# Last projection of a two-layer recurrent trunk: token parts of 384 and 128, and another way to 1/rms

## The chip, the cores and the metric

The kernel runs on one core of a Trainium2 chip. The metric is the time of one execution on the device in microseconds (us). A core has a matrix engine (TensorE, PE in the profile; its weight loads are PEld), a vector engine (VectorE, DVE), a scalar engine (ScalarE, ACT), a general one (GpSimd, POOL), and SyncE (SP), which here issues the transfers between the chip's memory and the core's SBUF. Matmuls write into PSUM, in banks of 512 fp32 columns.

## What is computed

A trunk of two layers over 512 tokens of width 2048, with residual adds and a final RMSNorm. The change lies at the very end, in layer 1's output projection, its residual add and the final norm:

```python
x = x + ssd_layer(rmsnorm(x, o_norm[j]), ...)   # ends in: return y @ w_out, y: 512 x 4096, w_out: 4096 x 2048
return rmsnorm(x, final_norm)

def rmsnorm(x, w):
    y = xf * lax.rsqrt(jnp.mean(xf * xf, axis=-1, keepdims=True) + EPS)
    return y * w
```

The mean is over the 2048 features of one token, and the whole product must be known for a token before any of its features can be scaled.

## The kernel before

Everything is held transposed: features on the 128 partitions, tokens along the free axis. The residual `x` is `acc_t`, 16 column tiles (`acc[0]` to `acc[15]`) of 128 features by 512 tokens. A weight matrix comes from memory in fp32, and ScalarE and VectorE split it into a rounded part and the rest (`split`, L167 to L169), both in the type fp32r; the moving operand is split likewise. `mm3` (L146 to L150) then multiplies with three matmuls: high by high, high by low, low by high. Each of the three loads its 128 x 128 weights first. Matmuls on plain fp32 tiles stand in the trace as two instructions each.

Layer 1 works through eight groups of features. The output projection of a group, 512 of the 4096 inputs, is added into `acc` while the next group is computed (`outproj`). For the last group nothing follows that could hide it, and so it is written apart, from L890 to the end of `trunk`:

- The 16 weight tiles `wl` are loaded and split ahead of time.
- `out_tile(j, lo, hi)` makes 12 matmuls (four input tiles times three) for column tile `j` and tokens `lo` to `hi` into a PSUM bank `po`, adds them to `acc[j]` (`evac`, VectorE, L217), squares the result (ScalarE, L910), adds the squares into `ssq2` (L912), and multiplies `acc[j]` by its norm weight (ScalarE, L915).
- Column tiles 0 to 7 (`FULL`) go over all 512 tokens, and GpSimd adds their squares. Tiles 8 to 15 then go over tokens 0 to 255, and after that over 256 to 511; VectorE adds those squares.
- After each half a matmul with a matrix of ones sums `ssq2` over the partitions and puts the sum on all of them (`rs`, L925 and L926). ScalarE takes the root (`std`, L928), VectorE the reciprocal of 128 x 256 values in two pieces (L180), and then VectorE scales the 16 tiles in five products (L933), each followed by a transfer of 256 or 512 KB to `out`.

The first half's scaling and output run while TensorE does the second half. Each engine runs its instructions in one order, fixed when the program is built; a tile framework adds the waits. `evac` is placed with high priority, so on VectorE the adds of the second half stand between the products of the first. All transfers of the end go through SyncE's one queue, in program order: a transfer whose data are not ready holds up those behind it.

Of the kernel before, what the change touches and what calls it, by code (L numbers as in the profile page):

```python
# [9 lines left out]
F32 = mybir.dt.float32  # L10
F32R = mybir.dt.float32r
AF = mybir.ActivationFunctionType
# [4 lines left out]
P = 128  # L17
S = 512
D = 2048
KD = D // P  # L20
# [23 lines left out]

VB = (2, 2)

FULL = 8

WARM = 7
QS = [(6, 10)] * (NG - 1) + [(4, 6)]  # L50
# [3 lines left out]
def trunk(ctx, tc, x_t, par, w_in0, w_qkvo, w_lru, w_if, w_out0, w_in1, w_out1, out):  # L54
    nc = tc.nc
    v, sc, gp, pe = nc.vector, nc.scalar, nc.gpsimd, nc.tensor
    MUL, ADD, SUB, MAX, MIN = ALU.mult, ALU.add, ALU.subtract, ALU.max, ALU.min
# [7 lines left out]
    def dma(o, i):  # L65
        return nc.sync.dma_start(o, i)
# [3 lines left out]
    def pc(name, j=0, n=1):  # L70
        o = OFF[name][0] + j
        return prm[:, o:o + n]

    ident = pc("ident", 0, 128)
    mask = pc("mask", 0, 128)
    eps = cst.tile([P, 1], F32, name="eps")
# [4 lines left out]
    aiT = cst.tile([P, 16], F32, name="aiT")  # L81
# [3 lines left out]
    r_bc = cst3.tile([P, S], F32, name="r_bc")  # L85
    acc_t = cst3.tile([P, KD, S], F32, name="acc")
    acc = [acc_t[:, k] for k in range(KD)]
# [5 lines left out]
    ones = ones_r.bitcast(F32)  # L93
# [5 lines left out]
    def next_raw():  # L99
        raw_i[0] += 1  # L100
        return raws[raw_i[0] % len(raws)]
# [44 lines left out]
    def mm3(ps, w, mov, first, last):  # L146
        (wh, wl), (mh, ml) = w, mov
        pe.matmul(ps, wh, mh, start=first, stop=False)  # L148
        pe.matmul(ps, wh, ml, start=False, stop=False)  # L149
        pe.matmul(ps, wl, mh, start=False, stop=last)  # L150
# [20 lines left out]
    def mmt(name="mm"):  # L171
        return pmm.tile([P, S], F32, tag="mm", name=name)

    def axt(name="ax"):
        return pax.tile([P, S], F32, tag="ax", name=name)


    def recip(dst, src, w=S):
        for o in range(0, w, P):
            v.reciprocal(dst[:, o:o + P], src[:, o:o + P])  # L180
# [34 lines left out]
    def evac(o, a, b, op):  # L215
        with tc.high_priority(offset=1000):
            v.tensor_tensor(o, a, b, op=op)  # L217
# [41 lines left out]
    def st(name="s", dt=F32):  # L259
        return sp[0].tile([P, S], dt, tag="s", name=name, bufs=sp[1])  # L260
# [30 lines left out]
    for k in range(KD):  # L291
# [10 lines left out]
        hi = wp.tile([P, 512], F32R, tag="whi", name="whi", bufs=4)  # L302
        lo = wp.tile([P, 512], F32R, tag="wlo", name="wlo", bufs=4)
        o = 512 * (k % 2)
# [17 lines left out]
        for w, m in ((hi, xh), (hi, xl), (lo, xh)):  # L322
            for t in range(4):
                pe.matmul(ps01[t], w[:, t * P:(t + 1) * P], m[k], start=(k == 0 and w is hi and m is xh),
                          stop=(k == KD - 1 and w is lo))
# [10 lines left out]
    def xslot(name):  # L336
        return (PA.tile([P, S], F32R, tag="yh", name=name + "h", bufs=8),
                PA.tile([P, S], F32R, tag="yl", name=name + "l", bufs=8))
# [17 lines left out]
    for h in range(NH):  # L356
        xm, xc = [], []
        for t in range(4):
            j = 4 * h + t
            if h:  # L360
                ps = mmt("xm")
                proj(ps, w_in0[16 + j], xpairs)
            else:
                ps = ps01[j]
# [288 lines left out]
    ps = mmt("dt")  # L653
    wdt = []
    for c in range(2):
        with tc.high_priority(offset=3000):
            w = next_raw()[:, 3:]
# [4 lines left out]
    hs = [(slice(64 * e, 64 * e + 64), slice(256 * e, 256 * e + 256)) for e in range(2)]  # L662
# [12 lines left out]
    def lt(tag, bufs=1, shape=(P, S), dt=F32):  # L675
        return L1.tile(list(shape), dt, tag=tag, name=tag, bufs=bufs)
# [211 lines left out]
    wl = []  # L888
# [1 line left out]
        wl += load_w(w_out1[j // 2, NG - 1], (xpairs[j], xpairs[j + 1]) if j < KD - 2 else (None, None))  # L890


    H = S // 2
    ssq2 = st("ssq2")
    sqs = {}

    def out_tile(j, lo, hi):
        n = hi - lo
        pst = mmt("po")
        for kk in range(4):  # L900
            ks = slice(kk * P, (kk + 1) * P)
            y = prev["out"][kk]
            mm3(pst[:, :n], (wl[j][0][:, ks], wl[j][1][:, ks]), (y[0][:, lo:hi], y[1][:, lo:hi]), kk == 0, kk == 3)
        a = acc[j][:, lo:hi]
        evac(a, a, pst[:, :n], ADD)
        if j == 0:
            sc.activation(ssq2, a, AF.Square)
        else:
            sq = st("sq")[:, :n]
            sc.activation(sq, a, AF.Square)  # L910
            if j < KD - 1:
                (gp if n == S else v).tensor_tensor(ssq2[:, lo:hi], ssq2[:, lo:hi], sq, op=ADD)  # L912
            else:
                sqs[lo] = sq
        sc.mul(a, a, pc("f_norm", j))  # L915

    for j in range(FULL):
        out_tile(j, 0, S)
    for hf in range(2):
        hs = slice(hf * H, (hf + 1) * H)  # L920
        for j in range(FULL, KD):
            out_tile(j, hf * H, (hf + 1) * H)
        r = r_bc[:, hs]
        ps = axt("rs")
        pe.matmul(ps[:, :H], ones, ssq2[:, hs], start=True, stop=False)  # L925
        pe.matmul(ps[:, :H], ones, sqs[hf * H], start=False, stop=True)  # L926
        std = st("std")[:, :H]
        sc.activation(std, ps[:, :H], AF.Sqrt, bias=eps, scale=1.0 / D)  # L928
        recip(r, std, H)
        done = 0  # L930
        for n in (4, 4, 4, 2, 2):
            a = acc_t[:, done:done + n, hs]
            v.tensor_tensor(a, a, r.unsqueeze(1).to_broadcast([P, n, H]), op=MUL)  # L933
            dma(out[hf, :, done:done + n], a)
            done += n


def _cm(vec):
# [93 lines left out]
```

## Time and profile before

| | |
|---|---|
| median of 3 runs | 2637.56 us (2636.6 to 2639.3) |
| the profiled execution | 2636.36 us |
| its span, first to last instruction | 2634.5 us |
| mean granted TensorE clock | 0.998 |
| column tile 4 of the last projection begins | 2584.38 us |
| tile 8, tokens 0 to 255, begins | 2595.26 us |
| last matmul of the projection starts | 2619.32 us |
| first scaled product of the second half starts | 2625.34 us |

Times inside the execution are counted from the start of its span. In the groups of instructions the figures behind the bar are the total busy time in us, the mean of one in ns, and the idle time just before them with what ended it. "x6" counts instructions. Matmuls are pipelined: their records overlap, so the distance from one start to the next, not the record's length, is what one costs.

### The profile page before, as it was taken

How to read it: one execution, taken by the hardware profiler on the slowest of the kernel's cores; microseconds unless marked ns; L12 is line 12 of the kernel's file. 1: busy time of each engine (PE TensorE's matmuls, PEld its weight loads, DVE VectorE, ACT ScalarE, POOL GpSimd, SP SyncE). 2: the span in 40 equal slices, each digit the busy share in tenths (PEclk: the TensorE clock that was granted, in tenths of full speed). 3: DMA queues.
4: the chain of work that ended last, by engine and by line, in shares of the span. 5: the costliest groups of instructions: out<-in, count | busy, mean ns of one | idle time of the engine just before them, and what ended most of it. 6: DMA issues, size and time to landing. Idle time of an engine off the chain costs nothing.

```text
span 2634.5 us, 32622 instructions
## 1 busy us (share of the span) xinstructions
PE 2619.1 (99%) x12246; PEld 2147.1 (81%) x12246; DVE 1642.9 (62%) x2708; ACT 1190.4 (45%) x1846; POOL 97.8 (4%) x86
## 2 busy tenths in 40 slices
PE   9999999999999999999999999999999999999997
PEld 8887878788888888888888888888888888888887
DVE  8452534487757757665767666666666666666676
ACT  6443443477436446453554334343343333343435
POOL 1000000000000000000200000000000000000001
PEclk9999999999999999999999999999999999999999
DMA  5424242533333323332253332323333333233332
GB/s 184 137 96 144 96 136 96 161 102 129 113 106 112 115 102 108 102 108 96 85 132 113 104 120 96 120 101 108 112 101 115 105 104 120 90 123 101 107 104 105
DMA packets 114910, 297.18 MB, mean 113 GB/s; under 512 B 11960, under 2 KB 35256, under 8 KB 114752
## 3 DMA queue, kind: packets, MB, share of 16 engines
q1 hardware_dynamic: 114608, 294.83, 34.0%
q8 instruction: 97, 1.59, 0.2%
q14 instruction: 61, 0.50, 0.1%
q10 hardware_dynamic: 144, 0.26, 0.0%
HBM read 277.99 MB, written 17.06 MB: 112 GB/s over the span
## 4 chain that ended last, share of the span: by engine, by line
PE 99%; DMA 0%; DVE 0%; ACT 0%; SPq 0%; issue 0%; DVEq 0%
PE po L148 9%; PE po L149 9%; PE po L150 9%; PE xbc L148 7%; PE xbc L150 7%; PE xbc L149 7%; PE z L148 4%; PE z L150 4%; PE z L149 4%; PE xl L148 2%; PE xl L149 2%; PE zm L148 2%; PE zm L149 2%; PE xl L150 2%; PE zm L150 2%; PE zl L150 2%
## 5 line engine op out<-in xcount | busy, mean ns | idle before, releaser
L168 ACT CAST whi<-wraw 128x512 fp32r<-128x512 f32 (+1 forms) x881 | 541.3, 615 | 1073.8 <-PE po L149 285.1
L169 DVE TENSOR_TENSOR wlo<-wraw,whi 128x512 fp32r<-128x512 f32 (+1 forms) x881 | 622.5, 707 | 520.2 <-ACT whi L168 490.3
L148 PE MATMUL xbc<-xh,whi 128*128 128x512 f32 x768 | 300.9, 392 | 0.0
L150 PE MATMUL xbc<-xh,wlo 128*128 128x512 f32 x768 | 299.0, 389 | 0.0
L149 PE MATMUL xbc<-xl,whi 128*128 128x512 f32 x768 | 298.9, 389 | 0.0
L217 DVE TENSOR_TENSOR acc<-acc,po 128x512 f32<-128x512 f32 (+1 forms) x264 | 175.8, 666 | 187.7 <-PE po L150 186.9
L148 PE MATMUL z<-xh,whi 128*128 128x512 f32 x512 | 206.9, 404 | 0.0
L150 PE MATMUL z<-xh,wlo 128*128 128x512 f32 x512 | 199.8, 390 | 0.0
L149 PE MATMUL z<-xl,whi 128*128 128x512 f32 x512 | 199.3, 389 | 0.0
L148 PE MATMUL po<-yh,whi 128*128 128x512 f32 (+1 forms) x456 | 179.4, 393 | 0.0
L150 PE MATMUL po<-yh,wlo 128*128 128x512 f32 (+1 forms) x456 | 176.9, 388 | 0.0
L149 PE MATMUL po<-yl,whi 128*128 128x512 f32 (+1 forms) x456 | 176.7, 388 | 0.0
L148 PEld LDWEIGHTS xbc<-xh,whi 128*128 128x128 f32 x768 | 144.2, 188 | 30.6 <-issue 1.2
L150 PEld LDWEIGHTS xbc<-xh,wlo 128*128 128x128 f32 x768 | 144.2, 188 | 30.1
L149 PEld LDWEIGHTS xbc<-xl,whi 128*128 128x128 f32 x768 | 144.2, 188 | 29.5
L235 POOL TENSOR_TENSOR ssq<-ssq,sq 128x512 f32<-128x512 f32 x51 | 65.9, 1292 | 1598.1 <-ACT sq L234 1598.1
L150 PEld LDWEIGHTS z<-xh,wlo 128*128 128x128 f32 x512 | 96.1, 188 | 20.9
L149 PEld LDWEIGHTS z<-xl,whi 128*128 128x128 f32 x512 | 96.3, 188 | 20.5 <-issue 1.9
L148 PEld LDWEIGHTS z<-xh,whi 128*128 128x128 f32 x512 | 96.3, 188 | 20.4 <-issue 2.1
L148 PE MATMUL zl<-xh,whi 128*128 128x512 f32 x256 | 101.5, 396 | 0.0
L148 PE MATMUL po<-ylh,whi 128*128 128x512 f32 x256 | 100.9, 394 | 0.0
L150 PEld LDWEIGHTS po<-yh,wlo 128*128 128x128 f32 x456 | 85.6, 188 | 18.0
(342 smaller groups left out, 5216.6 us busy)
## 6 DMA issues: line engine op xcount, KB each, us to landing
wraw<-in_w_in_dram SPq DMA_DIRECT2D x287, 512.0 KB, 3.2
wraw<-in_w_out_dram SPq DMA_DIRECT2D x128, 512.0 KB, 3.2
dab<-dad SPq DMA_DIRECT2D x64, 256.0 KB, 3.2
wraw<-in_w_qkvo_dram SPq DMA_DIRECT2D x24, 512.0 KB, 3.2
E<-ed SPq DMA_DIRECT2D x64, 128.0 KB, 2.9
vd<-vn SPq DMA_DIRECT2D x16, 256.0 KB, 3.7
od<-zm SPq DMA_DIRECT2D x16, 256.0 KB, 3.8
V<-vd SPq DMA_DIRECT2D x16, 256.0 KB, 3.9
```

The source lines that it names most:

```text
L148: pe.matmul(ps, wh, mh, start=first, stop=False)
L149: pe.matmul(ps, wh, ml, start=False, stop=False)
L150: pe.matmul(ps, wl, mh, start=False, stop=last)
L168: last_hi[:] = [sc.copy(hi, src)]
L169: return v.tensor_tensor(lo, src, hi.bitcast(F32), op=SUB)
L217: v.tensor_tensor(o, a, b, op=op)
L235: eng.tensor_tensor(ssq, ssq, sq, op=ADD)
```

## The change

Up to column tile 3 of the last projection every engine's order is as before. From there:

- `FULL` is 4 and a new constant `TA` is 384. Column tiles 0 to 3 go over 512 tokens, tiles 4 to 15 over tokens 0 to 383, all in one loop; GpSimd adds the squares of both.
- Tokens 384 to 511 of tiles 4 to 15 come last, in three groups of four column tiles. A group shares one PSUM bank, 128 columns for each tile, and has one add, one square (`ssqB`, `sqB`) over 512 columns and four products with the norm weight.
- The sum of squares is taken with the squares as weights and one column of ones as the moving operand (`r_sum`): the sums stand with tokens on partitions, one column for every 128 tokens. The squares of the last tiles go into it directly. Root and reciprocal work on 3 columns (first part) or 1 (second).
- `r_rows` brings 1/rms back to rows: ScalarE scales the identity by it (`dg`), and a matmul of ones with that diagonal puts it on all partitions, in PSUM (`rb`).
- `scale` copies `rb` to SBUF (`rc`) and scales. GpSimd does tiles 0 to 2 of the first part and group 0 of the second from the copy; VectorE does the rest from PSUM. The second part's results go to buffers of their own (`xdt`, `Pt`).
- The output tensor has the first part's 16 x 384 columns and then the second's 16 x 128; the host puts them together.

TensorE, where the first half ended before: `rs` sums over tokens, `po` is the projection.

```order
L150 MATMUL po<-xh_96,wlo 128x256
L925 MATMUL rs<-ssq_20562,ones_r 128x256
L148 MATMUL po<-yh,xh_89 128x256
L149 MATMUL po<-yl,xh_89 128x256
L150 MATMUL po<-yh,xl_105 128x256
L148 MATMUL po<-yh,xh_89 128x256
L149 MATMUL po<-yl,xh_89 128x256
L926 MATMUL rs<-sq,ones_r 128x256
L150 MATMUL po<-yh,xl_105 128x256
```

TensorE now, behind the first 24 matmuls of the 128-token part (column tiles 4 and 5); `rt` is the sum with tokens on partitions.

```order
L151 MATMUL po<-xl_112,xh_86 128x128
L152 MATMUL po<-xh_96,xl_102 128x128
L910 MATMUL rt<-ones_r,ssq_20562 128x1
L910 MATMUL rt<-ones_r,sq 128x1
L910 MATMUL rt<-ones_r,ssq_20562 128x1
L910 MATMUL rt<-ones_r,sq 128x1
L910 MATMUL rt<-ones_r,ssq_20562 128x1
L910 MATMUL rt<-ones_r,sq 128x1
L150 MATMUL po<-yh,xh_87 128x128
L151 MATMUL po<-yl,xh_87 128x128
```

The first part's sum moved from directly behind its last tile to 24 matmuls further on, and `rb` (three matmuls) stands another 24 behind it.

VectorE's last instructions before, from the add of tile 14's second half on.

```order
L217 TENSOR_TENSOR acc<-acc,po 128x256
L912 TENSOR_TENSOR ssq_20562<-ssq_20562,sq 128x256 x3
L217 TENSOR_TENSOR acc<-acc,po 128x256
L912 TENSOR_TENSOR ssq_20562<-ssq_20562,sq 128x256 x3
L180 RECIPROCAL r_bc<-std 128x128 x2
L933 TENSOR_TENSOR acc<-acc,r_bc 128x4x256 x3
L933 TENSOR_TENSOR acc<-acc,r_bc 128x2x256 x2
```

VectorE's last instructions now, from the adds of the 384-token tiles on.

```order
L219 TENSOR_TENSOR acc<-acc,po 128x384 x12
L912 RECIPROCAL aiT<-aiT 128x3
L219 TENSOR_TENSOR acc<-acc,po 128x4x128
L927 TENSOR_TENSOR acc<-acc,rb 128x3x384 x3
L927 TENSOR_TENSOR acc<-acc,rb 128x2x384 x2
L219 TENSOR_TENSOR acc<-acc,po 128x4x128 x2
L912 RECIPROCAL aiT<-aiT 128x1
L927 TENSOR_TENSOR xdt<-acc,rb 128x512
L927 TENSOR_TENSOR Pt<-acc,rb 128x512 x2
```

No sum of squares is left on VectorE, the reciprocals shrink to 3 and 1 columns, and three products stand at the end where five stood.

SyncE's output transfers now, behind the last weights.

```order
L68 DMA wraw<-in_w_out_dram 128x1024 x11
L68 DMA out_dram<-acc 128x3x384 x4
L68 DMA out_dram<-acc 128x2x384 x2
L68 DMA out_dram<-xdt 128x512 x2
L68 DMA out_dram<-Pt 128x512 x2
```

Their number stays at ten, now six for the first part and four for the second. The first of each part, one of the four `acc` rows and one of the two `xdt` rows, is that of GpSimd's product.

The diff, cut to its core:

```diff
-FULL = 8
+FULL = 4
+
+TA = 384
...
-    H = S // 2
-    ssq2 = st("ssq2")
-    sqs = {}
-
-    def out_tile(j, lo, hi):
-        n = hi - lo
-        pst = mmt("po")
+    ssq2, ssqB = st("ssq2"), lt("ssq")
+    aB = acc_t[:, :, TA:]
+
+    def out_tile(pst, j, lo, hi):
         for kk in range(4):
...
+    def r_sum(parts, rs):
+        pt = axt("rt")
+        for b in range(len(parts)):
+            for i, q in enumerate(parts[b]):
+                pe.matmul(pt[:, b:b + 1], q, ones[:, 0:1], start=i == 0, stop=i == len(parts[b]) - 1)
+        sc.activation(rs, pt[:, :len(parts)], AF.Sqrt, bias=eps, scale=1.0 / D)
+        v.reciprocal(rs, rs)
+
+    def r_rows(rs, n):
+        dg, rp = st("dg"), axt("rb")
+        for b in range(n):
+            bs = slice(b * P, (b + 1) * P)
+            sc.mul(dg[:, bs], ident, rs[:, b:b + 1])
+            pe.matmul(rp[:, bs], ones, dg[:, bs], start=True, stop=True)
+        return rp[:, :n * P]
+
+    def scale(rp, w, tiles):
+        c = st("rc")[:, :w]
+        sc.copy(c, rp)
+        for eng, rr, o, a, dst in tiles(c, rp):
+            eng.tensor_tensor(o, a, rr.unsqueeze(1).to_broadcast([P, a.shape[1], w]), op=MUL)
+            dma(dst, o)
+
+    for j in range(KD):
+        w = S if j < FULL else TA
+        pst = mmt("po")
+        out_tile(pst[:, :w], j, 0, w)
...
+        if 0 < j < KD - 1:
+            gp.tensor_tensor(ssq2[:, :w], ssq2[:, :w], sq, op=ADD)
         sc.mul(a, a, pc("f_norm", j))
-
-    for j in range(FULL):
-        out_tile(j, 0, S)
-    for hf in range(2):
-        hs = slice(hf * H, (hf + 1) * H)
-        for j in range(FULL, KD):
-            out_tile(j, hf * H, (hf + 1) * H)
-        r = r_bc[:, hs]
-        ps = axt("rs")
-        pe.matmul(ps[:, :H], ones, ssq2[:, hs], start=True, stop=False)
-        pe.matmul(ps[:, :H], ones, sqs[hf * H], start=False, stop=True)
-        std = st("std")[:, :H]
-        sc.activation(std, ps[:, :H], AF.Sqrt, bias=eps, scale=1.0 / D)
-        recip(r, std, H)
...
+    rA, rB = aiT[:, 0:TA // P], aiT[:, 4:5]
+    sqB = None
+    for g in range(FULL, KD, 4):
+        pst = mmt("po")
+        for t in range(4):
+            out_tile(pst[:, t * P:(t + 1) * P], g + t, TA, S)
+            if (g, t) == (FULL, 1):
+                r_sum([[q[:, b * P:(b + 1) * P] for q in (ssq2, sq)] for b in range(TA // P)], rA)
+        if g == FULL:
+            rpA = r_rows(rA, TA // P)
+        a, p3 = aB[:, g:g + 4], pst.rearrange("p (j n) -> p j n", n=P)
+        evac(a, a, p3, ADD)
+        sqB = ssqB if g == FULL else st("sqB")
+        sc.activation(sqB.rearrange("p (j n) -> p j n", n=P), a, AF.Square)
+        if FULL < g < KD - 4:
+            gp.tensor_tensor(ssqB, ssqB, sqB, op=ADD)
+        for t in range(4):
+            sc.mul(aB[:, g + t], aB[:, g + t], pc("f_norm", g + t))
+        if g == FULL:
+            def tiles_a(c, rp):
+                for lo, hi, eng, rr in ((0, 3, gp, c), (3, 6, v, rp), (6, 9, v, rp), (9, 12, v, rp),
+                                        (12, 14, v, rp), (14, 16, v, rp)):
...
+            scale(rpA, TA, tiles_a)
+    r_sum([[ssq2[:, TA:]] + [q[:, t * P:(t + 1) * P] for q in (ssqB, sqB) for t in range(4)]], rB)
+    rpB = r_rows(rB, 1)
+    obs = [lt("xdt", 2, (P, 4, P)), lt("xdt", 2, (P, 4, P)), lt("Pt", 2, (P, 4, P)), lt("Pt", 2, (P, 4, P))]
+
+    def tiles_b(c, rp):
+        for g, eng, rr in ((0, gp, c), (1, v, rp), (2, v, rp), (3, v, rp)):
...
+    scale(rpB, P, tiles_b)
```

More of the change, by code (lines that the diff above doesn't have):

```diff
@@ L902, in out_tile @@
             y = prev["out"][kk]
[L903 to L914, printed above, removed]
@@ L915, in out_tile @@
-        sc.mul(a, a, pc("f_norm", j))
-    for j in range(FULL):
-        out_tile(j, 0, S)
-    for hf in range(2):
-        hs = slice(hf * H, (hf + 1) * H)
-        for j in range(FULL, KD):
-            out_tile(j, hf * H, (hf + 1) * H)
-        r = r_bc[:, hs]
-        ps = axt("rs")
-        pe.matmul(ps[:, :H], ones, ssq2[:, hs], start=True, stop=False)
-        pe.matmul(ps[:, :H], ones, sqs[hf * H], start=False, stop=True)
-        std = st("std")[:, :H]
-        sc.activation(std, ps[:, :H], AF.Sqrt, bias=eps, scale=1.0 / D)
-        recip(r, std, H)
[L930 to L935, printed above, removed]
+            mm3(pst, (wl[j][0][:, ks], wl[j][1][:, ks]), (y[0][:, lo:hi], y[1][:, lo:hi]), kk == 0, kk == 3)
@@ new lines, in scale @@
+    def scale(rp, w, tiles):
[8 more added lines that the diff above has]
+        out_tile(pst[:, :w], j, 0, w)
+        a = acc[j][:, :w]
+        evac(a, a, pst[:, :w], ADD)
+        sq = ssq2 if j == 0 else st("sq")[:, :w]
+        sc.activation(sq, a, AF.Square)
+        if 0 < j < KD - 1:
+            gp.tensor_tensor(ssq2[:, :w], ssq2[:, :w], sq, op=ADD)
+        sc.mul(a, a, pc("f_norm", j))
@@ new lines, in trunk @@
+    rA, rB = aiT[:, 0:TA // P], aiT[:, 4:5]
[20 more added lines that the diff above has]
+                                        (12, 14, v, rp), (14, 16, v, rp)):
+                    a = acc_t[:, lo:hi, :TA]
+                    yield eng, rr, a, a, out[:, lo * TA:hi * TA].rearrange("p (j n) -> p j n", n=TA)
+            scale(rpA, TA, tiles_a)
@@ new lines, in trunk @@
+    r_sum([[ssq2[:, TA:]] + [q[:, t * P:(t + 1) * P] for q in (ssqB, sqB) for t in range(4)]], rB)
[3 more added lines that the diff above has]
+        for g, eng, rr in ((0, gp, c), (1, v, rp), (2, v, rp), (3, v, rp)):
+            o = out[:, KD * TA + g * S:KD * TA + (g + 1) * S].rearrange("p (j n) -> p j n", n=P)
+            yield eng, rr, obs[g], aB[:, 4 * g:4 * g + 4], o
+    scale(rpB, P, tiles_b)
@@ L1025 @@
         args.append(nc.dram_tensor(f"in_{name}_dram", a.shape, F32, kind="ExternalInput").ap())
-    args.append(nc.dram_tensor("out_0_dram", (2, P, KD, S // 2), F32, kind="ExternalOutput").ap())
+    args.append(nc.dram_tensor("out_0_dram", (P, KD * S), F32, kind="ExternalOutput").ap())
     with tile.TileContext(nc) as tc:
@@ L1030 @@
     o = r.results[0]["out_0_dram"]
-    return np.ascontiguousarray(o.transpose(0, 3, 2, 1)).reshape(1, S, D)
+    o = np.concatenate([o[:, :KD * TA].reshape(P, KD, TA), o[:, KD * TA:].reshape(P, KD, S - TA)], axis=2)
+    return np.ascontiguousarray(o.transpose(2, 1, 0)).reshape(1, S, D)
```

## Prediction

> **What bounds the kernel now.** I read the profile page first, for its head and the busy times:
>
> ```profile
> span 2634.5 us, 32622 instructions
> PE 2619.1 (99%) x12246; PEld 2147.1 (81%) x12246; DVE 1642.9 (62%) x2708; ACT 1190.4 (45%) x1846; POOL 97.8 (4%) x86
> ```
>
> TensorE is busy all along, so its stream counts until it ends, and after that the chain behind it. The instruction order shows nothing moved ahead of column tile 4 of the last projection, so I asked for the busy times by stage from there (columns: stretch, its length, PE, PEld, DVE, ACT, POOL busy, granted clock, DMA share, GB/s):
>
> ```profile
> 2584.38:2595.30 10.92, 10.92 (x50) 9.05 (x49) 4.05 (x6) 7.31 (x12) 6.20 (x5) 1.00 0.00 0
> 2595.30:2606.80 11.50, 11.50 (x97) 11.42 (x95) 6.28 (x15) 7.59 (x16) 1.59 (x2) 1.00 0.01 2
> 2606.80:2619.45 12.65, 12.57 (x102) 12.32 (x100) 10.34 (x19) 5.56 (x13) 0.00 (x0) 1.00 0.45 158
> 2619.45:2625.34 5.89, 1.25 (x6) 0.68 (x4) 3.75 (x9) 3.10 (x8) 0.00 (x0) 0.87 0.06 22
> 2625.34:2630.04 4.70, 0.00 (x0) 0.00 (x0) 4.69 (x5) 0.00 (x0) 0.00 (x0) 0.50 0.58 206
> 2630.04:2634.50 4.46, 0.00 (x0) 0.00 (x0) 0.00 (x0) 0.00 (x0) 0.00 (x0) 0.50 0.72 254
> ```
>
> Three stretches of matmuls (tiles 4 to 7 of 512 tokens, then both halves of 256), then 15 us in which TensorE does next to nothing. The timeline gives the ends of these stretches:
>
> ```profile
> 2584.38 0.39 PE L148 MATMUL po<-yh,xh 128*128 128x512 f32 x1
> ...
> 2595.26 0.28 PE L148 MATMUL po<-yh,xh 128*128 128x256 f32 x1
> 2595.37 0.28 PE L149 MATMUL po<-yl,xh 128*128 128x256 f32 x1
> ...
> 2619.32 0.28 PE L150 MATMUL po<-xh,wlo 128*128 128x256 f32 x1
> ```
>
> A 512 matmul takes (2595.26 - 2584.38)/48 = 0.227 us, a 256 one 0.12 us. The chain of waits shows what stands between the last product and the end:
>
> ```profile
> 2621.32 0.44 DVE ssq L912
> 2621.89 0.67 PE rs L925 x2
> 2623.03 0.48 ACT std L928
> 2623.54 1.77 DVE r_bc L180 x2
> 2625.34 1.23 DVE acc L933
> 2626.56 1.13 DVEq L1027
> ```
>
> and the DMA columns, 1 us at a time, what the output does:
>
> ```profile
> 2627.00:2628.00 1.00, 0.00 (x0) 0.00 (x0) 1.00 (x2) 0.00 (x0) 0.00 (x0) 0.50 0.50 180
> ...
> 2632.00:2633.00 1.00, 0.00 (x0) 0.00 (x0) 0.00 (x0) 0.00 (x0) 0.00 (x0) 0.50 1.06 373
> 2633.00:2634.00 1.00, 0.00 (x0) 0.00 (x0) 0.00 (x0) 0.00 (x0) 0.00 (x0) 0.50 0.02 4
> ```
>
> The half's output (128 x 16 x 256 floats, 2.1 MB) begins to flow at about 2627.55, 0.95 us behind the first scaled product (2625.34 + 1.23), flows for 5.45 us at 0.38 MB per us, and the span ends 1.5 us behind its last byte. So the end is the first product plus a transfer, and the DVE products after the first cost nothing.
>
> **TensorE's part of the change.** Tiles 4 to 15 now run 144 matmuls of 384 tokens, then 144 of 128. The first size stands elsewhere in the trace, in the attention's `num`:
>
> ```profile
> 569.92 0.33 PE L148 MATMUL num<-Ph,vh 128*128 128x384 f32 x1
> 570.10 0.34 PE L149 MATMUL num<-Pl,vh 128*128 128x384 f32 x1
> 570.27 0.34 PE L150 MATMUL num<-Ph,vl 128*128 128x384 f32 x1
> 570.45 0.29 PE L148 MATMUL num<-Ph,vh 128*128 128x256 f32 x1
> ```
>
> 0.53/3 = 0.177; halfway between the 512 and the 256 pitch would be 0.173. I take 0.175: 25.2 us.
>
> No split-precision (fp32r) matmul of 128 tokens is in the trace, so this is the price to bound. The columns alone would give 0.12 - 128 x (0.227 - 0.12)/256 = 0.067 us. But each matmul brings its own 128-column weight load, and the load rows say how long one occupies the path (last figure: mean ns of one):
>
> ```profile
> L149 PEld LDWEIGHTS xbc<-xl,whi 128*128 128x128 f32 x768 | 144.2, 188 | 29.5
> L815 PEld LDWEIGHTS yo<-Ct,xw 128*128 128x128 f32 x192 | 26.3, 190 | 2.5
> ```
>
> ```profile
> L784 PEld LDWEIGHTS yd<-Pt,xdt 128*64 128x64 f32 x512 | 27.3, 136 | 11.3 <-issue 4.6 <-PE z L149 3.5 <-PE po L149 2.5
> ```
>
> 64 columns more cost 52 ns, so 128 columns occupy about 104 ns of the 188, for fp32r (`xbc`) as for plain fp32 (`yo`). Behind a plain fp32 stretch two fp32r loads follow each other as closely as they can:
>
> ```profile
> 2524.34 0.19 PEld L148 LDWEIGHTS z<-xh,whi 128*128 128x128 f32 x1
> 2524.45 0.19 PEld L149 LDWEIGHTS z<-xl,whi 128*128 128x128 f32 x1
> ```
>
> 0.11 us apart. And plain fp32 instructions with the very same shapes, 128 x 128 weights and 128 columns, run at:
>
> ```profile
> 2523.78 0.83 PE L815 MATMUL yo<-Ct,xw 128*128 128x128 f32 x6
> ```
>
> ```profile
> L815 PE MATMUL yo<-Ct,xw 128*128 128x128 f32 x24 | 3.3, 274 | 0.0
> ```
>
> Three products are six instructions there, each 0.27 us from start to end, so the pitch is (0.83 - 0.27)/5 = 0.112 us. So the bounds are 0.067 (loads hidden) and 0.120 (no cheaper than 256 tokens); I take 0.112, the row with the same shapes: 144 x 0.112 = 16.1 us. The 128-token part then costs nearly what a 256-token part costs, for half the tokens: that is the change's own price.
>
> The operations around the matmuls I price from their groups by form (the figure behind the comma is again the mean ns of one):
>
> ```profile
> L217 DVE TENSOR_TENSOR acc<-acc,po 128x512 f32<-128x512 f32 x20 | 13.5, 681 | 13.2 <-PE po L150 13.0
> ...
> L915 ACT ACTIVATE acc<-acc,prm 128x256 f32<-128x256 f32 x16 | 7.9, 505 | 0.4
> ...
> L915 ACT ACTIVATE acc<-acc,prm 128x512 f32<-128x512 f32 x8 | 5.7, 722 | 0.2
> L910 ACT ACTIVATE sq<-acc 128x512 f32<-128x512 f32 x7 | 4.4, 632 | 5.6 <-DVE acc L217 5.5
> ...
> L180 DVE RECIPROCAL r_bc<-std 128x128 f32<-128x128 f32 x4 | 3.7, 935 | 3.7 <-ACT std L928 3.7
> ```
>
> ```profile
> L912 POOL TENSOR_TENSOR ssq<-ssq,sq 128x512 f32<-128x512 f32 x7 | 9.4, 1337 | 38.8 <-issue 30.5 <-ACT sq L910 8.3
> ```
>
> Into this part go the first 1/rms (`rt`, 6 products, and `rb`, 3), plain fp32, hence two instructions each like `yo`: 18 x 0.112 = 2.0 us, plus 0.15 us for each of the two switches. That figure is from the second half above: 12.65 us less 96 x 0.12 leaves 1.13 for four `rs` instructions of 256 columns at 0.213, so 0.28 for two switches. Sum 2.3 us. I give no wait to TensorE in this part, because the order leaves 24 matmuls, 2.7 us, ahead of `rt` and again ahead of `rb`. Ahead of `rt` stand tile 15's add and square, about 0.55 and 0.5 us by the rows for 512 columns; ahead of `rb` the root, the reciprocal and three diagonals, about 1.6 us. If loads turned out hidden, these 24 would last only 1.6 us and the cover would be just used up. The 384 tiles themselves are covered as well: of a tile's 2.1 us the dearest helper, GpSimd's add, takes 1.34 x 384/512 = 1.0.
>
> The new waits sit on ScalarE and SyncE. ScalarE's root waits for `rt` and its copy `rc` for `rb`; behind them in its queue stand the squares and the weight products of the 128-token groups, for which nobody waits until the next sum. `rb` is through at 2584.4 + 25.2 + 48 x 0.112 + 2.3 = 2617.3, the copy 0.5 later. VectorE's five products of the first part (13 tiles of 384 columns, at 0.68 for 512 at most 6.6 us) then run to 2624.4 at the latest, so the second group's add, ready at 2622.7, comes up to 1.7 late; three PSUM banks take that up, and the third group's add at 2628 finds VectorE free.
>
> TensorE's products thus end at 2584.38 + 25.2 + 16.1 + 2.3 = 2628.0, against 2619.45: **8.55 us later**.
>
> **The tail.** The last matmul is done 0.16 us behind the stream's end (0.28 less 0.12). Then follow, one behind the other:
>
> - add of four column tiles, 512 columns: 0.68
> - their square: 0.63
> - `rt`: of its 18 instructions eight need the last square. They start 0.15 behind it (as `rs` behind `ssq` in the chain) and take 7 x 0.112 + 0.27, together 1.2. Beside them ScalarE has four weight products of 128 columns, 4 x 0.3 + 0.1 = 1.3 by the slope of L915, ahead of the root in its queue. So 1.3.
> - root of one column: 0.48 (L928 in the chain, 256 columns) less 255 x 0.00085, the slope of L915, 0.26; reciprocal of one column: at most 0.1, since 0.935 is for 128
> - diagonal, 128 columns: 0.505 - 128 x 0.00085 = 0.40
> - `rb`, two instructions: 0.15 + 0.11 + 0.27 = 0.53
> - copy of `rb` to SBUF: 0.3 (L910 at 128 columns)
> - GpSimd's product of 512 columns: 1.34
> - five handovers of 0.03 (2623.03 + 0.48 against 2623.54)
>
> That is 5.7, and GpSimd's product is done at 2633.85. It stands first in SyncE's queue of output transfers, so VectorE's three products, the first of them done 0.65 earlier, wait behind it: GpSimd buys nothing here, and costs 0.65. Then 0.95 to the first byte, 1.05 MB at 0.38, 2.75, and 1.5: the end is at **2639.1**.
>
> What leaves the tail is real: 15.05 us behind the stream's end become 11.1, 3.95 less, of which 2.7 is the smaller transfer. But 8.55 is lost ahead of it: **+4.6**. The first part's 3.1 MB are hidden: its GpSimd product (1152 columns, 1.34 x 1152/512 = 3.0 us), first in SyncE's queue, ends near 2620.8, so the bytes flow from 2621.7 to 2630, before the last part's from 2634.8. If they came later than that, each microsecond would count whole.
>
> Against this execution's 2636.4 us (span and 1.9 around it), the sum gives 2641.0; it lies 1.2 below the median of the three runs, 2637.56, so I add the 4.6 to the median: **2642.2 us**. A measurement of this kernel can tell about 0.2%, 5.3 us, from no change, so this is "the same" by a narrow margin. Bounds: 0.108 to 0.120 for the pitch, -0.6 to +1.2; 0.173 to 0.177 for the 384 pitch, 0.3 each way; the tail 1 each way. Alone: 2640.3 to 2644.7.
>
> **Rivals.** *Loads overlap* (10%). The load records of 188 ns already overlap at a pitch of 0.12 in the halves, so two may be under way and the columns set the pace: 144 x 0.067 = 9.6, 6.5 less. The first part's transfer would then end at 2627.7 and the last part's start at 2628.3, so all of it counts: -1.9, 2635.7 us. Against it speak the 0.11 us between the two `z` loads. The Trainium skill has two rules here, in "TensorE: Matmul & The Clock Gate": section "Back-to-back issue gap" gives about 81 ns for load and matmul of 128 columns in a stream, and "Weight-path perf modes" has fast weight load on for every type but FP32. By 81 ns the second part would be an estimated 11.7 us and the end 0.1 us behind that of before. The trace shows no faster load for fp32r, 188 against 190 ns; no run yet shows the pitch.
>
> *Narrow fp32r falls to the rate of plain fp32* (16%), the case on the slower side. Every fp32r row in the trace has 256, 384 or 512 columns; where the attention has a 128-column piece it uses plain fp32. If such a matmul needs the two passes that plain fp32 shows, it costs 2 x 0.112 = 0.224: 16.1 more, +20.7, 2658.3 us. It decides from a pitch of about 0.117 up, where the sum passes 5.3. Against it: the pitch falls evenly from 512 to 256, without a step.
>
> *GpSimd's product is slow* inside the main case: all four transfers queue behind it, so if the copy and the product took 1 us longer, beside a busy VectorE, the end would be at +5.6. This is in the tail's bound.
>
> **Chances.** That the loads bound the pitch has the rest, 74%, of which nearly 4 in 10 lie above +5.3 (0.27); with the narrow case, slower 0.43. Faster by 5.3 needs more than the loads rival gives: 0.04. Same 0.53. The range reaches down to the loads rival, 2635.0, and up to 2647.0, leaving out mainly the narrow case.
>
> **What would show it.** Right: a `po` 128x128 matmul every 0.11 us with back-to-back loads, the last at 2628, the output 1.05 MB in under 3 us, end near 2639. Wrong: a pitch of 0.07 or 0.22; TensorE idle at `rt` or `rb`; the transfer starting before GpSimd's last product; first-part bytes still flowing at 2634.

## The result, and the profile after

The changed kernel takes 2653.38 us (median of 5 runs, 2651.99 to 2655.24); the kernel before, on the same chip, 2637.56. The ratio is 1.0062, with a 95% interval of 1.0051 to 1.0072: 16 us slower, where 4.6 were forecast, and above the range of 2635 to 2647. The profiled execution took 2652.04 us, its span 2650.2. One execution of the twelve of experiment e4 below took 4434.44 us at a mean granted clock of 0.556, where the other eleven took 2636.68 to 2639.09 at 0.997 or more; no trace of it was kept, and the ratio given there leaves it out.

The 128-token part first ran as the prediction said. The timeline of TensorE at its start and 6 us into it (start, duration, instruction):

```profile
2608.57 0.33 PE L152 MATMUL po<-xh,wlo 128*128 128x384 f32 x1
2608.74 0.22 PE L150 MATMUL po<-yh,xh 128*128 128x128 f32 x1
2608.80 0.27 PE L151 MATMUL po<-yl,xh 128*128 128x128 f32 x1
2608.91 0.27 PE L152 MATMUL po<-yh,xl 128*128 128x128 f32 x1
...
2611.37 0.33 PE L910 MATMUL rt<-ones_r,ssq 128*128 128x1 f32 x2
...
2612.45 0.36 PE L910 MATMUL rt<-ones_r,sq 128*128 128x1 f32 x2
...
2614.83 0.28 PE L151 MATMUL po<-xl,xh 128*128 128x128 f32 x1
2614.94 0.29 PE L152 MATMUL po<-xh,xl 128*128 128x128 f32 x1
2615.05 0.39 PE L150 MATMUL po<-xh,xh 128*128 128x128 f32 x1
2615.24 0.42 PE L151 MATMUL po<-xl,xh 128*128 128x128 f32 x1
2615.46 0.42 PE L152 MATMUL po<-xh,xl 128*128 128x128 f32 x1
...
2637.22 0.41 PE L152 MATMUL po<-xh,wlo 128*128 128x128 f32 x1
```

The part starts at 2608.74 (forecast: 2584.38 + 25.2 = 2609.6) with a matmul every 0.11 us. From 2615.05 one takes 0.213. No wait stands there; the busy times by stage show what changed (columns as before: stretch, length, PE, PEld, DVE, ACT, POOL busy, granted clock, DMA share, GB/s):

```profile
2614.00:2615.00 1.00, 1.00 (x11) 1.00 (x11) 0.00 (x0) 0.40 (x2) 0.00 (x0) 1.00 0.00 0
2615.00:2616.00 1.00, 1.00 (x7) 1.00 (x7) 0.09 (x1) 0.00 (x0) 0.00 (x0) 0.53 0.00 0
2616.00:2618.00 2.00, 2.00 (x11) 2.00 (x11) 0.74 (x2) 0.65 (x2) 0.09 (x1) 0.50 0.00 0
2618.00:2624.00 6.00, 6.00 (x31) 6.00 (x30) 5.48 (x5) 1.64 (x5) 2.56 (x1) 0.50 0.45 168
```

The granted clock goes from 1.00 to 0.50 at 2615.06, while TensorE is busy 1.00 of every us, and stays there. In 6.3 us 45 of the 144 matmuls had started; the other 99 cost 0.101 more each, 10.0 us. The last one starts at 2637.22.

The tail, from the timeline of all engines:

```profile
2637.43 2.23 PE L910 MATMUL rt<-ones_r,ssq 128*128 128x1 f32 x10
2637.67 0.69 DVE L219 TENSOR_TENSOR acc<-acc,po 128x512 f32<-128x512 f32 x1 [9.55 <-PE po L152]
2638.39 0.63 ACT L954 ACTIVATE sqB<-acc 128x512 f32<-128x512 f32 x1 [8.30 <-DVE acc L219]
...
2639.53 1.84 PE L910 MATMUL rt<-ones_r,sqB 128*128 128x1 f32 x8
2641.41 0.26 ACT L911 ACTIVATE aiT<-rt,eps 128x1 f32<-128x1 f32 x1 [1.08 <-PE rt L910]
...
2642.41 0.79 PE L919 MATMUL rb<-dg,ones_r 128*128 128x128 f32 x2 [1.04 <-ACT dg L918]
2643.30 0.27 ACT L925 COPY rc<-rb 128x128 f32<-128x128 f32 x1 [0.94 <-PE rb L919]
2643.60 0.69 DVE L927 TENSOR_TENSOR xdt<-acc,rb 128x512 f32<-128x512 f32 x1 [1.73 <-ACT rc L925]
2643.64 1.27 POOL L927 TENSOR_TENSOR xdt<-acc,rc 128x512 f32<-128x512 f32 x1 [13.50 <-ACT rc L925]
...
2644.94 0.82 SPq L68 DMA_DIRECT2D out_dram<-xdt  x2
```

GpSimd's product is done at 2644.91, VectorE's first at 2644.29, and the first transfer is issued at 2644.94: it waited for GpSimd. From there to the span's end are 5.26 us (forecast 0.95 + 2.75 + 1.5 = 5.2).

So the miss of 11.1 us (2650.2 against 2639.1) has three pieces: the narrow part began 0.84 earlier than forecast; from 2608.74 to its end, 2637.43, it took 28.7 instead of 16.1 + 2.3 = 18.4, 10.3 more; and the tail took 12.8 instead of 11.1.

### The profile page after: what moved, and what is told of

Read it like the earlier page. It is cut to its first block, busy times and chain, and to the rows that moved or that the text cites. A ratio compares the mean times of both kernels' runs of the same rounds, so it can differ in the third digit from the quotient of the medians.

```text
span 2650.2 us, 32779 instructions
## 1 busy us (share of the span) xinstructions
PE 2640.3 (100%) x12324; PEld 2171.1 (82%) x12324; DVE 1632.1 (62%) x2685; ACT 1191.7 (45%) x1851; POOL 108.4 (4%) x96
## 4 chain that ended last, share of the span: by engine, by line
PE 99%; DMA 0%; DVE 0%; ACT 0%; SPq 0%; DVEq 0%; issue 0%; ACTq 0%
PE po L150 9%; PE po L152 9%; PE po L151 9%; PE xbc L150 7%; PE xbc L152 7%; PE xbc L151 7%; PE z L150 4%; PE z L152 4%; PE z L151 4%; PE xl L150 2%; PE xl L151 2%; PE zl L150 2%; PE zl L152 2%; PE zl L151 2%; PE zm L152 2%; PE xl L152 2%
```

## The experiments

What lowered the clock? Theory A: the stream of 128-column matmuls itself, which fills the array for only half of the time. Theory B: the twelve one-column `rt` instructions in it. `rb` starts at 2615.67, behind the fall, and is out.

**The first part's sums behind the stream** (e1). The calls of `r_sum`, `r_rows` and `scale` for the first part move behind the loop over the groups:

```diff
-            if (g, t) == (FULL, 1):
-                r_sum([...], rA)
-        if g == FULL:
-            rpA = r_rows(rA, TA // P)
...
+    r_sum([...], rA)
+    rpA = r_rows(rA, TA // P)
...
```

> The first part's 1/rms and its products are moved behind the whole stream of 128-token tiles, so that nothing but 128-column fp32r matmuls stands in that stream. Theory A (the stream itself lowers the clock: a 128-column matmul every 0.112 us keeps the array busy for only about half the time): the granted clock still falls to 0.5 some 6 us after the stream begins, that is near 2615, the pitch goes from 0.112 to 0.213, and the last po matmul starts near 2634.6 (2637.2 less the 2.6 us of rt and rb that stood in the stream). Theory B (the twelve rt instructions of one column, 1.3 us, trip it): the clock stays at 1.00, the pitch at 0.112, and the last po matmul starts at 2608.7 + 16.1 = 2624.8. The time as a whole is later than with the sums in between in both, since the first part's products and transfer then come last: about 2655 to 2660 by A, 2647 to 2652 by B.

Measured, in one execution: 2651.18 us. Two stretches of the stream:

```profile
2608.00:2616.00 8.00, 8.00 (x72) 8.00 (x70) 1.24 (x2) 2.79 (x7) 1.02 (x1) 1.00 0.00 0
2616.00:2624.00 8.00, 8.00 (x74) 8.00 (x73) 0.69 (x1) 2.84 (x9) 1.28 (x1) 1.00 0.01 3
...
2624.00:2628.00 4.00, 2.84 (x24) 2.76 (x24) 0.86 (x2) 1.73 (x6) 0.00 (x0) 0.92 0.00 0
```

The clock holds to the end of the stream, whose last matmul starts at 2624.67 (B: 2624.8). A falls.

**The first part's sum in the old form** (e2): ones as weights, 384 columns, at the same place; the first part's products then read `r_bc`, so its `rb` and its copy go too.

```diff
-                r_sum([...], rA)
+                psA = axt("rs")
+                pe.matmul(psA[:, :TA], ones, ssq2[:, :TA], start=True, stop=False)
+                pe.matmul(psA[:, :TA], ones, sq, start=False, stop=True)
...
+                sc.activation(stdA, psA[:, :TA], AF.Sqrt, bias=eps, scale=1.0 / D)
+                recip(r_bc[:, :TA], stdA, TA)
-        if g == FULL:
-            rpA = r_rows(rA, TA // P)
...
```

> The first part's 1/rms is taken in the form that the kernel before has (ones as weights, 384 columns, result on all partitions), at the same place in the stream: no one-column rt and no rb there; the second part's sum stays as changed. Theory A (the 128-column stream lowers the clock): the fall comes within about 2 us of where it was, 2615, the stream's second half again has a pitch of 0.213, the last po matmul starts near 2636 and the time is within 3 us of the changed kernel, 2650 to 2654. Theory B (the one-column rt trips it): no fall, the last po matmul starts near 2608.7 + 16.1 + 1 = 2626, rt and rb of the second part take half as long, and the time is 2639 to 2641.

Measured: 2641.69 us, the median of ten, 0.7 above B's range; ratio to before 1.0018 (1.0009 to 1.0027). The clock holds to 2629.27, behind the last po matmul, which starts at 2628.20. This is B's case. It also lies near the prediction's 2642.2, and that is in part luck: the sum in the stream costs 1.2 here where the prediction has 2.3 for `rt` and `rb`, and the tail of the profiled execution (2644.04, one of the longer ones) takes 13.9 instead of 11.1.

**Narrow slices elsewhere** (e3), in the kernel before: four column tiles of an earlier projection in slices of 128 tokens.

```diff
-            chunk(ps, ws[j % 2], ys, 0, 4)
+            for i in range(4):
+                ts = slice(i * P, (i + 1) * P)
+                chunk(ps[:, ts], ws[j % 2], [(y[0][:, ts], y[1][:, ts]) for y in ys], 0, 4)
```

> The kernel before, with four column tiles of the last group's projection, in the middle of the last layer's work and far from any rt or rb, taken in four slices of 128 tokens each: 192 fp32r matmuls of 128 columns in place of 48 of 512. Theory A: the pitch is 0.112 for the first 4 to 8 us, then the granted clock halves and the pitch goes to 0.21; the 192 take (6.3 + 136 x 0.213 =) about 35 us in place of about 11, the clock comes back some us after 512-column matmuls run again, and the time is 20 to 30 us longer than before's. Theory B: no fall, 192 x 0.112 = 21.5 us, and the time is about 10 us longer.

Measured, in one execution: 2647.05 us, 10.2 above before's 2636.84. The last 144 of the 192 slices run at 0.112 on end, 16 us, at a clock of 1.00; the last full stretch of 4 us:

```profile
2469.00:2473.00 4.00, 4.00 (x39) 4.00 (x37) 1.00 (x2) 0.27 (x1) 0.00 (x0) 1.00 0.00 0
```

B's number again.

**The sizes undone, the rest kept** (e4): `FULL = 8`, `TA = 256`, two column tiles to a bank.

> The changed kernel with the sizes undone and the rest kept: eight tiles of 512, then parts of 256 and 256 tokens, two column tiles to a bank, the sums with tokens on partitions, GpSimd in the products of both parts. Theory A (what counts is how much of the time the columns fill the array, 0.107 of 0.12 us at 256): the clock stays at 1.00 through both parts, the rt of the first part included, and the time is that of before within 0.1%, 2635 to 2639. Theory B (rt trips it): the eight one-column rt instructions of the first part lower the clock for at least one stretch of 3 us, and the time is 2 to 6 us longer than before's.

Measured: ratio to before 1.0001 (0.9992 to 1.0009), clock 1.00 through both parts. Here the eight `rt` do nothing, against B. So the narrow stream alone leaves the clock up, and so do eight `rt` among wider matmuls. Twelve alone aren't shown by this run; what is left to try is whether it takes the two together.

**Doses of one-column work** in the narrow slices (f2) and between 512-column tiles (f3), with theory C (the clock follows the mean number of columns over a stretch of time) against D (it takes a run of more than eight one-column instructions, whatever stands around it). Here is what comes on top of the slices of e3:

```diff
+            if slices and j in (1, 2):
+                dz = axt("rt")
+                for _ in range(3 * j):     # f3: 6 * j, and no slices
+                    pe.matmul(dz[:, 0:1], ones, ones[:, 0:1], start=True, stop=True)
```

> The kernel with the four sliced tiles in the middle of the last layer (192 matmuls of 128 columns, no fall there), plus extra one-column plain fp32 matmuls whose result nobody uses: six instructions behind the second sliced tile, twelve behind the third. Theories C and D both: the clock falls some 2.5 to 4 us after the start of the twelve; C allows, D excludes, that the six (0.67 us, a mean of about 930 columns per us over 3.7 us) do it already. Behind the slices come 512-column matmuls again: the clock comes back there within some 4 us if a fall is undone by a well-used stretch. With the fall only behind the twelve, of the last 48 slices about half run at 0.213, and the time is 10.2 + 2 + 2 to 5 us longer than before's, about 2651 to 2654.

Measured, in one execution: 2656.66 us. The six, at 2463.35, do nothing; the twelve, from 2469.38, are followed by the fall at 2471.35. It came sooner than either theory had it, 2.0 us behind the first of the twelve, and the way back later, which fits a time above the forecast. The busy times in stretches of 3.413 us, laid so that one boundary is the fall:

```profile
2461.09:2464.51 3.42, 3.42 (x33) 3.42 (x32) 0.96 (x2) 0.62 (x1) 0.00 (x0) 1.00 0.02 5
2464.51:2467.92 3.41, 3.41 (x33) 3.41 (x32) 0.33 (x1) 0.00 (x0) 0.00 (x0) 1.00 0.42 154
2467.92:2471.33 3.41, 3.41 (x33) 3.41 (x33) 1.29 (x2) 0.62 (x1) 0.00 (x0) 1.00 0.00 0
2471.33:2474.75 3.42, 3.42 (x18) 3.42 (x18) 0.00 (x0) 0.00 (x0) 0.00 (x0) 0.50 0.00 0
2474.75:2478.16 3.41, 3.41 (x18) 3.41 (x18) 0.00 (x0) 0.00 (x0) 0.00 (x0) 0.50 0.00 0
2478.16:2481.57 3.41, 3.41 (x15) 3.22 (x15) 0.96 (x2) 0.62 (x1) 0.00 (x0) 0.50 0.00 0
2481.57:2484.99 3.42, 3.42 (x9) 2.65 (x9) 0.33 (x1) 0.00 (x0) 0.00 (x0) 0.50 0.45 153
2484.99:2488.40 3.41, 3.41 (x29) 2.62 (x29) 2.46 (x5) 0.62 (x1) 0.00 (x0) 1.00 0.02 5
```

Why 3.413: the clock comes back at 2485.00, 13.65 us behind the fall, and falls once more in the tail at 2642.01, 157.01 behind the return. These are 4.00 and 46.0 times 3.413. The other traces agree: in the changed kernel the clock is up from 3.86 to 2615.06, which is 765.0 times 3.4133. The Trainium skill says so in "TensorE: Matmul & The Clock Gate", section "What's actually happening": a window of 3413 ns that runs freely and isn't tied to the kernel's start. On this the trace agrees. The same section has the half clock come behind an idle window; here TensorE is busy in the whole of 2467.92 to 2471.33, and the clock falls at its end, so the measurement goes further than the page.

> The kernel before, not sliced, with one-column plain fp32 matmuls whose result nobody uses between 512-column tiles at the same place: twelve instructions behind the second tile, 24 (2.7 us) behind the third. Theory C: the twelve leave a mean of 2300 x 2.4 / 3.7 = 1500 columns per us, as the eight did within 256 columns, and do nothing; 24 leave about 2300 x 1.0 / 3.7 = 620 at the worst and lower the clock to 0.5 for some 3.5 us. Theory D: the twelve lower it already.

Measured, in one execution: 2640.78 us, no fall, not even behind the 24, a miss for both C and D. The run of 24 rules D out. C is saved only if the mean isn't a sliding one but is taken over fixed stretches: then a boundary at 2463.33 (counted back in steps of 3.4133 from this run's fall in the tail, 2627.17) cut the 24, which ran from 2461.84 to 2464.43, into 15 and 9. (The expectation of the 48 below says 17 and 10; the trace has 24 in all.) That is theory E: the clock is decided at the end of each fixed stretch by the columns in it. f1 ran beside f2 and f3, and E was made from all three; f1b, g1 and g3 came after it and test it.

**`rt` spread** (f1, and once more as f1b): four behind each of three 128-token tiles; `rb` and the first part's products come a group later.

```diff
-            if (g, t) == (FULL, 1):
-                r_sum([...], rA)
-        if g == FULL:
-            rpA = r_rows(rA, TA // P)
+            if g == FULL and t:
...
+                for i, q in enumerate((ssq2, sq)):
+                    pe.matmul(ptA[:, t - 1:t], q[:, bs], ones[:, 0:1], start=i == 0, stop=i == 1)
...
+            if (g, t) == (FULL + 4, 1):
+                rpA = r_rows(rA, TA // P)
...
```

> The changed kernel with the first part's twelve rt instructions spread: four behind each of three tiles of 128 tokens, 12 po matmuls between them; root and rb then one group later. Three runs came before this: the 128-column stream alone held the full clock for 16 us (the first theory, that the stream itself lowers it, is out), eight rt within 256-column tiles did no harm, twelve within the 128-column stream did. Theory C (the clock follows the columns that the array took over a stretch of some 3.7 us; 128 each 0.112 us is 1143 per us, against about 2300 of the wide tiles; the fall in the changed kernel came after 3.7 us with 1.3 us of rt in it, a mean of about 740): here any 3.7 us hold at most 8 or 9 rt, a mean of about 850. Either the threshold lies below that, the clock stays at 1.00, and the time is 2640 to 2643, or it lies between 850 and 1143, the clock falls, and it is 2650 or later. Theory D (it takes a run of more than eight one-column instructions, whatever stands around it): no run is longer than four, no fall, 2640 to 2643.

> The spread rt once more, four behind each of three 128-token tiles, which gave 2644.5 once and 2653.4 to 2655.5 three times. By theory E a stretch that holds two whole groups of four (8 rt, 0.345) lowers the clock, one that holds fewer does not: groups 1.79 us apart and 0.45 long fall whole into one stretch for about 7 in 10 of the phases. So again most executions near 2654, some near 2643, and none between. A fixed cause that does not depend on the phase would give one value.

Measured: 2655.53, 2644.49, 2654.06 and 2653.44; then 2643.20, 2653.91, 2655.07 and 2653.74 us. One program, two values, none between; the longer one in six of eight, with a mean granted clock of 0.993 in these six and 0.998 in the other two. D expected no fall here, and C one value. The two traces happen to hold one of each. First f1, in stretches laid to its fall, then f1b, laid to its fall in the tail:

```profile
2610.97:2614.39 3.42, 3.42 (x31) 3.42 (x29) 0.56 (x1) 1.94 (x4) 1.02 (x1) 1.00 0.00 0
2614.39:2617.80 3.41, 3.41 (x33) 3.41 (x33) 0.00 (x0) 0.00 (x0) 0.00 (x0) 1.00 0.00 0
2617.80:2621.21 3.41, 3.41 (x18) 3.41 (x18) 0.86 (x2) 1.94 (x7) 0.00 (x0) 0.50 0.01 2
```

```profile
2610.26:2613.67 3.41, 3.41 (x34) 3.41 (x32) 0.00 (x0) 0.67 (x2) 0.00 (x0) 1.00 0.00 0
2613.67:2617.09 3.42, 3.42 (x33) 3.42 (x32) 0.86 (x2) 1.29 (x4) 0.00 (x0) 1.00 0.00 0
2617.09:2620.50 3.41, 3.41 (x32) 3.41 (x31) 0.00 (x0) 1.66 (x6) 0.00 (x0) 1.00 0.03 7
```

In f1 two groups of four lie well inside the stretch from 2614.39 (they start at 2614.49 and 2616.28). In f1b the boundary at 2613.67 falls into the last instruction of the second group, which starts at 2613.36: the stretch ahead of it holds all eight starts too, but 23 matmuls of 128 columns where f1's holds 22. So the phase decides, and f1b stands just beside the edge. By the count in the table below, a boundary near the middle of the twelve `rt` would spare the changed kernel too, in an estimated one execution of ten; all five had a mean granted clock of 0.993, so all five fell.

**Half of `rt`** (g1): GpSimd adds the last tile's square too; the sum comes a tile later, `rb` and the first part's products a group later.

```diff
-        if 0 < j < KD - 1:
+        if 0 < j:
...
-            if (g, t) == (FULL, 1):
-                r_sum([[q[:, b * P:(b + 1) * P] for q in (ssq2, sq)] for b in range(TA // P)], rA)
+            if (g, t) == (FULL, 2):
+                r_sum([[ssq2[:, b * P:(b + 1) * P]] for b in range(TA // P)], rA)
...
```

> The changed kernel with half the rt in the 128-token stream: GpSimd adds the last tile's square to the sum too, so six one-column instructions in place of twelve, one tile later; rb and the first part's products one tile and one group later. Theory E, from the windows of all traces so far: the clock is decided at the end of each of a row of fixed stretches of 3.413 us by the columns that TensorE took in it, of at most 8192; it fell behind stretches with 0.345 and less, held at 0.391 and more. Six rt leave 0.39 in any phase, so the clock holds in every execution: 2640 to 2644 each time, the last po matmul near 2627.5 in the profile. Rival F (any run of one-column work in the narrow stream is a gamble that some executions lose): at least one of the executions is above 2649.

Measured: 2643.12 us, ten executions from 2642.33 to 2643.55, ratio 1.0022 (1.0012 to 1.0031). All ten have a mean granted clock of 0.998, so none fell within the stream; F is out. The stretch with the six has 0.376 of the columns, a little less than the 0.39 forecast:

```profile
2612.11:2615.53 3.42, 3.42 (x33) 3.42 (x32) 0.17 (x1) 0.89 (x4) 0.00 (x0) 1.00 0.00 0
```

**48 one-column instructions between wide tiles** (g3): as f3, but only behind the third tile, 24 matmuls of two instructions each.

> The kernel before with 48 one-column plain fp32 instructions (5.4 us at full clock) between two 512-column tiles in the middle of the last layer. 24 of them did nothing there; by theory E because a stretch boundary cut them 17 and 10, and 0.50 of the columns were left. 48 leave at most 0.25 in one stretch, whatever the phase: the clock falls for one or two stretches, 3.4 or 6.8 us, and comes back behind the first one that 512-column matmuls fill at half clock (0.50 of the columns). Time 8 to 12 us above before's. If wide matmuls around the run protect it instead, the clock stays at 1.00 and the time is 5.4 us above.

Measured, in one execution: 2647.28 us, 10.4 above before. In stretches laid to the fall:

```profile
2463.63:2467.05 3.42, 3.42 (x33) 3.42 (x32) 0.17 (x1) 0.00 (x0) 0.00 (x0) 1.00 0.01 2
2467.05:2470.46 3.41, 3.41 (x13) 2.93 (x13) 0.00 (x0) 0.00 (x0) 0.00 (x0) 0.50 0.00 0
2470.46:2473.87 3.41, 3.41 (x10) 2.64 (x9) 0.27 (x1) 0.62 (x1) 0.00 (x0) 0.50 0.02 5
2473.87:2477.29 3.42, 3.42 (x28) 2.69 (x26) 1.29 (x3) 0.62 (x1) 0.00 (x0) 1.00 0.38 140
```

Busy throughout, the stretch of one-column work lowers the clock at its end; two stretches later it is back, as E said.

What E counts can be worked out from the rows. At the half clock 512 columns take 0.427 us, here in f2:

```profile
2481.33 0.63 PE L150 MATMUL xbc<-xh,wlo 128*128 128x512 f32 x1
...
2483.89 0.63 PE L150 MATMUL xbc<-xh,wlo 128*128 128x512 f32 x1
```

Six of them in 2.56 us are 1200 columns per us, so at twice the clock 2400, and 8192 in a stretch. The table sums the columns of the matmuls that start in a stretch (one narrow matmul more or less at the edge is 0.016). The changed kernel's row in it is this one:

```profile
2611.65:2615.06 3.41, 3.41 (x33) 3.41 (x32) 0.18 (x1) 1.25 (x4) 0.00 (x0) 1.00 0.00 0
```

| stretch | one-column matmuls in it | share of 8192 columns | clock behind it |
|---|---|---|---|
| narrow stream alone (e1, e3) | 0 | 0.47 to 0.48 | stays 1.00 |
| 256-column stream (e4) | 8 | 0.66 | stays 1.00 |
| f3, the one with most of the 24 | 15 | 0.50 | stays 1.00 |
| f2, the six | 6 | 0.39 | stays 1.00 |
| g1 | 6 | 0.38 | stays 1.00 |
| f1b | 8 | 0.36 | stays 1.00 |
| f1 | 8 | 0.345 | falls |
| changed kernel, 2611.65 to 2615.06 | 9 | 0.345 | falls |
| f2, the twelve | 12 | 0.28 to 0.30 | falls |
| g3 | 31 | 0.00 | falls |
| at half clock: narrow stream alone | 0 | 0.25 | stays 0.50 |
| at half clock: f2, narrow and wide | 0 | 0.34 | stays 0.50 |
| at half clock: g3 | 4 | 0.38 | stays 0.50 |
| at half clock: wide alone (f2, g3) | 0 | 0.50 | back to 1.00 |

The number of one-column matmuls doesn't order the rows (15 among wide matmuls do nothing, 8 or 9 in the narrow stream are enough), the share of columns does. Counted the same way over all 14 traces, the full clock ended 16 times, the falls in the tails included, each time behind a stretch with 0.345 or less; none of the other 10,731 stretches at full clock has less than 0.36.

**GpSimd in the last products.** g2 is g1 without it and without the copy in the second part, e5 is e4 without them. The edit of g2, whose `False` leaves out the copy:

```diff
-        for g, eng, rr in ((0, gp, c), (1, v, rp), (2, v, rp), (3, v, rp)):
+        for g, eng, rr in ((0, v, rp), (1, v, rp), (2, v, rp), (3, v, rp)):
...
-    scale(rpB, P, tiles_b)
+    scale(rpB, P, tiles_b, False)
```

> The same without GpSimd and without the copy of the row in the last part's four products: VectorE makes all four. By the prediction's step (GpSimd buys nothing and costs 0.65, and the copy stands ahead of it) the first output transfer starts 0.65 us earlier and rb's reader 0.3 earlier; the fourth product of VectorE (0.65) is behind three transfers of 0.7 and delays nothing. The time is 0.6 to 1 us less than with GpSimd, 2639.5 to 2643; the profile tells more than the time here. Rival (GpSimd's product takes work off VectorE that would be late): the same or later.

Measured: 2642.53 us, ratio to before 1.0021 (1.0011 to 1.0030); 0.6 below g1's median, but the intervals of g1 and g2 overlap, so the times alone don't tell them apart. The timelines do, g1's first:

```profile
2633.41 0.79 PE L919 MATMUL rb<-dg,ones_r 128*128 128x128 f32 x2 [1.04 <-ACT dg L918]
...
2634.64 1.27 POOL L927 TENSOR_TENSOR xdt<-acc,rc 128x512 f32<-128x512 f32 x1 [7.48 <-ACT rc L925]
...
2635.94 0.82 SPq L68 DMA_DIRECT2D out_dram<-xdt  x2
```

```profile
2633.69 0.79 PE L919 MATMUL rb<-dg,ones_r 128*128 128x128 f32 x2 [1.04 <-ACT dg L918]
2634.52 1.28 DVE L929 TENSOR_TENSOR xdt<-acc,rb 128x512 f32<-128x512 f32 x2 [1.38 <-PE rb L919]
2635.23 0.94 SPq L68 DMA_DIRECT2D out_dram<-xdt  x2
```

From `rb` to the first transfer it is 2.53 us with GpSimd and 1.54 without: 0.99 less, the 0.6 to 1 that was expected.

> The version that could beat both kernels: sizes as before (parts of 256 and 256), the sums with tokens on partitions, no GpSimd product and no copy in the last part's products. The version with GpSimd there came out level with before. The copy (about 0.35 us) and the wait for GpSimd's product (its two tiles of 256 columns take 1.3 us, 0.6 more than VectorE's first) leave the chain, VectorE has two products more to do behind it: about 0.5 to 1 us earlier than with GpSimd, 2636 to 2637, within 0.1% of before. All theories of the clock: no fall before the last matmul.

Measured: ratio to before 1.0001 (0.9992 to 1.0010). None of these versions came out measurably faster than the kernel before.

## Why the prediction was wrong

- **The step that failed** is the price of the narrow part, "144 x 0.112 = 16.1 us". The pitch was right, to the third digit; what failed is that it was taken for the whole part. It held for 45 matmuls, then the granted clock halved, and 99 ran at 0.213: 10.0 us of the miss of 11.1. The halving came behind the stretch from 2611.65 to 2615.06, in which the narrow stream and nine `rt` left 0.345 of the columns. The prediction had the column of the granted clock in front of it, at 1.00 through all three stretches of products, and took it as given.
- **The rival on the slower side** named a pitch of 0.22 and +20.7 us, but from two passes per matmul. It is refuted: the same matmuls ran at 0.112 for 6.3 us here and for 16 us in e1 and e3. That a pitch of 0.22 was listed under "wrong" was luck: it came about, for another reason.
- **The rival of overlapping loads** is refuted too: the pitch stayed at 0.112 where the columns alone would allow 0.067. The Trainium skill's 81 ns ("TensorE: Matmul & The Clock Gate", section "Back-to-back issue gap") doesn't hold for these fp32r matmuls.
- **`rt` and `rb`** were priced by their time, 2.3 us, and the order gave them no wait. Both nearly held (2.6 us, with `rb` at the half clock, and no wait), and both were beside the point: their cost was that they took no columns. Without them in this form the kernel came to 2641.69 (e2) and, with half of them, to 2643.12 (g1), against 2642.2 forecast. That these lie so near is in part luck, for e2 as said there; in g1 the narrow part takes 17.4 us to its end instead of 18.4, and the tail 14.4 instead of 11.1, since the first part's products, a group later, keep VectorE from the last add for 2.0 us.
- **The tail**, 12.8 instead of 11.1 us: `rt` and `rb` run at the half clock. The last eight `rt` took 1.84 instead of 1.06, they started 0.36 late behind the ten ahead of them, and `rb` took 0.79 instead of 0.53; together 1.4 of the 1.7. The prediction's rows of the tail show the granted clock at 0.87 and then 0.50 in the kernel before as well; its `rs` ran ahead of that fall. In e2, g1 and g2, where the clock held through the stream, the last eight `rt` and `rb` still came behind the fall in the tail (2629.27, 2629.18 and 2628.85), so most of this piece of the miss would stand without the other.
- **GpSimd buys nothing, costs 0.65**: right. The wait is 2644.29 to 2644.94, and g2 saves 0.99, the copy included.
- **The first part's transfer is hidden**: right. The DMA share in the 32 us from 2618 on, in 40 slices of 0.8 us, has the first part's bytes from about 2621 to 2630, as forecast, and the last part's from 2645:

```profile
DMA  0000599999999920000000000000000000299900
```

## What to carry to other kernels

A stream of narrow matmuls that bring their own weights (128 columns every 0.112 us, 0.47 of what full speed takes) stands close to the point where the granted clock halves; nine one-column matmuls, 1.0 us, in one stretch of it were enough, and once the clock was down, the stream at 0.25 didn't lift it again. When a change narrows matmuls, or puts sums with one moving column among them, add up the columns in any 3.4 us, at the worst phase: in this case the fall came at 0.345 of what full speed takes and less, and not at 0.36 and more. Spreading isn't a cure if two pieces still fit into one stretch; taking half of them away was.

## What the runs showed of the hardware

- The granted clock fell while TensorE was busy 100% of the time. What matched all the falls is the number of columns that streamed through in fixed stretches of 3.413 us, whose boundaries lie elsewhere in each execution. What exactly the chip counts wasn't measured; columns are what fits, with the edge between 0.345 and 0.360. One narrow matmul more or less in the count is 0.016, so the edge is known no closer than that.
- The way back asks for more than staying up: at the half clock 0.375 didn't bring it back, 0.50 did. A 128-column stream there reached 0.25, and stayed down: 22 us in the changed kernel.
- One program gave two times 10 us apart (f1, f1b). The one trace of each differs in the phase of these stretches; the other six executions have only their mean granted clock, 0.993 or 0.998, to go by.
- Fp32r matmuls of 128 columns keep to 0.112 us as long as the clock is up, 16 us on end in e3. Four column tiles cut into such slices cost 10.2 us more there; by the pitches it is 192 x 0.112 - 48 x 0.227 = 10.6.
